# Add, LayerNorm and affine on one core: 16-row loads and stores, each in two transfers of the even and the odd partitions

## The chip, the cores and the metric

The kernel runs on one core of a Trainium2 chip. The metric is the device time of one launch in microseconds (us), the median of several runs. A launch takes about 2 us longer than the span that its profile shows (243.2 us against a span of 241.3 us for the kernel before).

## The reference

```python
def reference(x, residual, gamma, beta, eps):      # x, residual: [16, 1024, 512] float32
    z = x + residual
    mean = np.mean(z, axis=-1, keepdims=True)
    var = np.var(z, axis=-1, keepdims=True)
    z_norm = (z - mean) / np.sqrt(var + eps)
    return (gamma * z_norm + beta).astype(np.float32)
```

There are 16,384 rows of 512 floats. On chip each of the 128 partitions holds 128 of them ("rows 0 to 127" below are the rows of one partition, 2 KB each). Two inputs of 33.55 MB are read and one output of 33.55 MB is written.

## The kernel before

All loads and stores go through one DMA queue, issued by the SyncE (SP) engine. `zbuf` holds 64 rows per partition: x is loaded there, the residual is added in place, the result is made in place, and it is stored from there. So the X load of rows s+64 must wait for the store of rows s. `rbuf` holds 32 rows of the residual. In the code, `P` is the 128 partitions, `D` the 512 floats of a row, `asked`, `added` and `done` count rows, and `STORE_LAG` is by how many rows a store stays behind the X loads that have been issued.

```python
BLOCK = 16
X_CHUNKS = [8] * 15 + [4, 4]
R_CHUNKS = [8] * 15 + [4, 4]
OUT_CHUNKS = [16] * 7 + [8, 4, 4]
GROUP = 4
Z_ROWS = 64
R_ROWS = 32
STORE_LAG = 40
# ... (cut)
def dram(t, lo, n):          # n consecutive rows of every partition: one run of n * 2 KB
    k = lo % BLOCK
    # ... (cut: a check)
    v = t[P * (lo - k) : P * (lo - k + BLOCK), :].rearrange("(p j) d -> p j d", p=P)
    return v[:, k : k + n, :].rearrange("p a b -> p (a b)")
# ... (cut)
def load_x(lo, n):
    nc.sync.dma_start(out=part(zbuf, Z_ROWS, lo, n), in_=dram(xf, lo, n))
def load_r(lo, n):
    nc.sync.dma_start(out=part(rbuf, R_ROWS, lo, n), in_=dram(rf, lo, n))
def store(lo, n):
    nc.sync.dma_start(out=dram(of, lo, n), in_=part(zbuf, Z_ROWS, lo, n))
# ... (cut: add on GpSimd, statistics on ScalarE, affine1 and affine2 on VectorE, 4 rows a group)
def store_due():
    nonlocal added, done
    while stores and (
        stores[0][0] + stores[0][1] <= asked - STORE_LAG or asked == total
    ):
        lo, n = stores.pop(0)
        while done < lo + n:
            added, done = next(steps)
        store(lo, n)

for lo, n in spans(X_CHUNKS):
    asked = lo + n
    # ... (cut: a check)
    load_x(lo, n)
    while loads_r and loads_r[0][0] + loads_r[0][1] <= asked:
        while added < loads_r[0][0] + loads_r[0][1] - R_ROWS:
            added, done = next(steps)
        load_r(*loads_r.pop(0))
    if lo == 0:
        spread()
    store_due()
```

## Time and profile before

| | before |
|---|---|
| median time | 243.16 us (243.11 to 243.18, 3 runs) |
| span of the profile | 241.3 us |
| queue 1 (all loads and stores) | 100.67 MB, 97.9% of 16 engines |
| VectorE, ScalarE, GpSimd busy | 74%, 75%, 60% |

The first lines are from the profile's page of the kernel before. "DMA" and "GB/s" divide the span into 40 slices; the queue lines give packets, megabytes and the share of the 16 DMA engines' time; the "DMA 62%" line is the chain of work that ended last; the GpSimd (POOL) line gives busy us, mean ns, and the idle time before it with what ended most of it; the last two give what is loaded or stored, its issuing queue, how often, the KB each, and the median us from issue to landing.

```profile
span 241.3 us, 1109 instructions
...
DMA  7999999999999999999999999999999999999992
GB/s 261 434 435 434 434 430 418 421 425 432 432 470 436 391 426 421 429 434 426 430 434 437 430 424 429 429 451 410 425 426 432 475 387 418 462 434 432 413 410 117
...
q1 hardware_dynamic: 6336, 100.67, 97.9%
q14 instruction: 9, 0.07, 0.1%
...
DMA 62%; ACT 16%; DVE 6%; POOL 6%; SPq 1%; issue 1%; DVEq 0%; POOLq 0%
...
L120 POOL TENSOR_TENSOR zbuf<-zbuf,rbuf 128x2048 f32<-128x2048 f32 x32 | 144.1, 4526 | 70.6 <-DMA rbuf<-in_residual_dram 69.6
...
zbuf<-in_x_dram SPq DMA_DIRECT2D x15, 2048.0 KB, 29.2
...
out_dram<-zbuf SPq DMA_DIRECT2D x7, 4096.0 KB, 28.6
```

The kernel is bound by its data movement: the DMA engines are busy from end to end, and the first compute engine waits for residual loads, not the reverse.

The next lines are the same kernel's SP engine in order of time (start, duration, what it issued), one period of the loop:

```profile
82.38 0.33 SPq L84 DMA_DIRECT2D zbuf<-in_x_dram  x1
82.80 0.38 SPq L87 DMA_DIRECT2D rbuf<-in_residual_dram  x1
83.28 0.38 SPq L90 DMA_DIRECT2D out_dram<-zbuf  x1
83.71 0.42 SPq L84 DMA_DIRECT2D zbuf<-in_x_dram  x1
84.23 0.39 SPq L87 DMA_DIRECT2D rbuf<-in_residual_dram  x1
```

The period is X, R, S, X, R: behind each store stand an X and a residual load of 2 MB each.

The last lines of before are its windows before the loop's first store lands, in the loop, and after it (start:end, length, busy time of each compute engine, clock, DMA share, GB/s). A whole wave of 16 packets of 32 KB is 0.5 MB, so a window of 120 us can be off by some 4 GB/s, and a short one by much more.

```profile
25.00:75.00 50.00, 0.00 (x0) 0.00 (x0) 49.69 (x82) 49.71 (x153) 45.14 (x11) 1.00 1.02 434
75.00:195.00 120.00, 0.00 (x0) 0.00 (x0) 96.86 (x157) 96.98 (x296) 73.45 (x17) 1.00 1.00 428
195.00:225.00 30.00, 0.00 (x0) 0.00 (x0) 27.76 (x45) 24.48 (x75) 14.29 (x4) 1.00 1.02 433
```

The rate hardly drops where loads and stores are mixed. Between 75 and 195 us no packet starts after a gap (packet records, described below).

Finer readings below are from the trace's packet records (start, duration, size of each packet). They do not name the DMA engine; packets were put on 16 engines by joining each to the one that ended just where it starts. The median packet took 309 ns for 8 KB, 611 to 612 ns for 16 KB and 1213 ns for 32 KB. Where several engines end a packet within a few ns of each other the joining is ambiguous, so what is said of a single engine is less certain than what is said of all 16. "Excess" is a packet's time over the median of its size, per engine (the sum over all packets divided by 16).

### The profile page before, as it was taken

Reading aid. Unit: us, or ns where it says so; the run is one execution under the profiler, and the core shown is the slowest. Engines: PE = TensorE matmul, PEld = TensorE weight load, DVE = VectorE, ACT = ScalarE, POOL = GpSimd, SP = SyncE. Lnnn points to the kernel's source line nnn. Section 1 sums busy time; section 2 is a strip of 40 time slices with the busy share of each in tenths; the row PEclk is TensorE's granted clock in tenths of the full one; section 3 lists DMA queues with packets and bytes.
Section 4 is the critical chain, followed back from the end, with each engine's and each line's share of the span. In section 5 each row is a group of like instructions: output and inputs, shape, how many; then the busy total and the mean of one; then the engine's idle time right before and its main releaser. Section 6 shows DMA issues by size and latency. Waiting matters only on the chain.

```text
span 241.3 us, 1109 instructions
## 1 busy us (share of the span) xinstructions
PE 4.1 (2%) x4; PEld 1.0 (0%) x4; DVE 178.5 (74%) x290; ACT 180.1 (75%) x546; POOL 144.3 (60%) x36
## 2 busy tenths in 40 slices
PE   3300000000000000000000000000000000000000
PEld 0000000000000000000000000000000000000000
DVE  0005999999999999899934999359991699969200
ACT  2009999999999999999709997099961999697000
POOL 0088988989889507894078940889209891860000
DMA  7999999999999999999999999999999999999992
GB/s 261 434 435 434 434 430 418 421 425 432 432 470 436 391 426 421 429 434 426 430 434 437 430 424 429 429 451 410 425 426 432 475 387 418 462 434 432 413 410 117
DMA packets 6349, 100.74 MB, mean 417 GB/s; under 512 B 706, under 2 KB 706, under 8 KB 708
## 3 DMA queue, kind: packets, MB, share of 16 engines
q1 hardware_dynamic: 6336, 100.67, 97.9%
q14 instruction: 9, 0.07, 0.1%
q10 hardware_dynamic: 4, 0.00, 0.0%
HBM read 67.11 MB, written 33.55 MB: 417 GB/s over the span
## 4 chain that ended last, share of the span: by engine, by line
DMA 62%; ACT 16%; DVE 6%; POOL 6%; SPq 1%; issue 1%; DVEq 0%; POOLq 0%
DMA rbuf<-in_residual_dram 34%; DMA out_dram<-zbuf 28%; ACT junk L131 9%; ACT junk L140 7%; POOL zbuf L120 6%; DVE zbuf L175 3%; DVE zbuf L161 3%; SPq L84 1%; ACT std L148 0%; SPq L87 0%; SPq L90 0%; DVEq L261 0%; DVE rstd L173 0%; POOLq L120 0%; DVEq L161 0%
## 5 line engine op out<-in xcount | busy, mean ns | idle before, releaser
L120 POOL TENSOR_TENSOR zbuf<-zbuf,rbuf 128x2048 f32<-128x2048 f32 x32 | 144.1, 4526 | 70.6 <-DMA rbuf<-in_residual_dram 69.6
L161 DVE SCALAR_TENSOR_TENSOR zbuf<-zbuf,nm,gamma_t 128x512 f32<-128x512 f32 x128 | 89.5, 746 | 44.4 <-issue 22.5
L131 ACT ACTIVATE junk<-zbuf 128x512 f32<-128x512 f32 x128 | 74.2, 580 | 38.9 <-POOL zbuf L120 38.9
L175 DVE SCALAR_TENSOR_TENSOR zbuf<-zbuf,rstd,beta_t 128x512 f32<-128x512 f32 x128 | 87.1, 743 | 1.2
L140 ACT ACTIVATE junk<-zbuf,nm 128x512 f32<-128x512 f32 x128 | 85.9, 671 | 0.0
L140 ACT ACTIVATION_READ_ACCUMULATOR junk<-zbuf,nm 128x1 f32 x128 | 24.0, 187 | 0.0
L131 ACT ACTIVATION_READ_ACCUMULATOR junk<-zbuf 128x1 f32 x128 | 23.9, 187 | 0.0
L148 ACT ACTIVATE std<-ssq,eps_t 128x4 f32<-128x4 f32 x32 | 8.5, 267 | 1.0
L173 DVE RECIPROCAL rstd<-std 128x4 f32<-128x4 f32 x32 | 5.6, 175 | 0.0
L186 ACT ACT_TABLE_LOAD x1 | 1.3, 1283 | 1.5 <-PEq L247 1.5
L190 PE MATMUL beta_t<-gb_row,ones 1*128 1x512 f32 x2 | 2.1, 1136 | 2.3 <-DMA gb_row<-in_beta_dram 2.3
L190 PE MATMUL gamma_t<-gb_row,ones 1*128 1x512 f32 x2 | 2.0, 1122 | 2.3 <-DMA gb_row<-in_gamma_dram 2.3
L104 DVE MEMSET ones<- 1x128 f32 x1 | 0.2, 165 | 0.8 <-PEq L247 0.8
L190 PEld LDWEIGHTS beta_t<-gb_row,ones 1*128 1x128 f32 x2 | 0.5, 308 | 3.9 <-DMA gb_row<-in_beta_dram 3.9
L190 PEld LDWEIGHTS gamma_t<-gb_row,ones 1*128 1x128 f32 x2 | 0.5, 308 | 2.2 <-issue 2.2
L247 POOL MEMSET const-float32-0.0<- 128x1 f32 x1 | 0.1, 99 | 0.2 <-issue 0.2
L186 ACT ACTIVATE warm<-eps_t 128x1 f32<-128x1 f32 x1 | 0.2, 203 | 0.0
L247 POOL MEMSET const-bfloat16-1.0<- 128x1 bf16 x1 | 0.1, 102 | 0.0
L247 POOL MEMSET const-uint8-127<- 128x1 uint8 x1 | 0.1, 102 | 0.0
L247 POOL MEMSET const-float32-1.0<- 128x1 f32 x1 | 0.1, 99 | 0.0
L106 DVE MEMSET eps_t<- 128x1 f32 x1 | 0.1, 59 | 0.0
## 6 DMA issues: line engine op xcount, KB each, us to landing
zbuf<-in_x_dram SPq DMA_DIRECT2D x15, 2048.0 KB, 29.2
rbuf<-in_residual_dram SPq DMA_DIRECT2D x15, 2048.0 KB, 29.9
out_dram<-zbuf SPq DMA_DIRECT2D x7, 4096.0 KB, 28.6
zbuf<-in_x_dram SPq DMA_DIRECT2D x2, 1024.0 KB, 32.3
rbuf<-in_residual_dram SPq DMA_DIRECT2D x2, 1024.0 KB, 32.3
out_dram<-zbuf SPq DMA_DIRECT2D x1, 2048.0 KB, 23.5
out_dram<-zbuf SPq DMA_DIRECT2D x2, 1024.0 KB, 16.7
gb_row<-in_gamma_dram ACTq DMA_DIRECT2D x1, 2.0 KB
```

Source lines behind the costliest of these rows:

```text
L84: nc.sync.dma_start(out=part(zbuf, Z_ROWS, lo, n), in_=dram(xf, lo, n))
L104: nc.vector.memset(ones, 1.0)
L120: nc.gpsimd.tensor_tensor(out=z, in0=z, in1=part(rbuf, R_ROWS, j0, n), op=ALU.add)
L131: nc.scalar.activation(out=junk, in_=zrow(j0 + k), func=ACT.Identity, scale=-inv_d, accum_out=nm[:, k : k + 1],)
L140: nc.scalar.activation(out=junk, in_=zrow(j0 + k), func=ACT.Square, bias=nm[:, k : k + 1], accum_out=ssq[:, k : k + 1],)
L148: nc.scalar.activation(out=std[:, :n], in_=ssq[:, :n], func=ACT.Sqrt, bias=eps_t[:, 0:1], scale=inv_d,)
L161: nc.vector.scalar_tensor_tensor(out=zrow(j0 + k), in0=zrow(j0 + k), scalar=nm[:, k : k + 1], in1=gamma_t, op0=ALU.add, op1=ALU.mult,)
L173: nc.vector.reciprocal(out=rstd[:, :n], in_=STD.pop(g)[:, :n])
L175: nc.vector.scalar_tensor_tensor(out=zrow(j0 + k), in0=zrow(j0 + k), scalar=rstd[:, k : k + 1], in1=beta_t, op0=ALU.mult, op1=ALU.add,)
L186: nc.scalar.activation(out=warm, in_=eps_t, func=ACT.Sqrt)
L190: nc.tensor.matmul(dest, ones, gb_row[:, k, :], start=True, stop=True)
L247: nc = _bacc.Bacc("TRN2", target_bir_lowering=False, num_devices=1)
```

## The change

The intent is fewer, larger packets: a packet is one partition's run, and with 16 rows it is 32 KB. A single 4 MB X load would need all of the old store to be out before it starts, so each 16-row transfer is cut into two of 2 MB, one of the even and one of the odd partitions: the even half of a load then waits only for the even half of the store.

```diff
-X_CHUNKS = [8] * 15 + [4, 4]
-R_CHUNKS = [8] * 15 + [4, 4]
+X_CHUNKS = [16] * 8
+R_CHUNKS = [8, 8] + [16] * 6 + [8, 4, 4]
 OUT_CHUNKS = [16] * 7 + [8, 4, 4]
@@
+    def transfer(out, in_, n):
+        parts = 2 if n == BLOCK else 1
+        for h in range(parts):
+            nc.sync.dma_start(out=out[h::parts, :], in_=in_[h::parts, :])
+
     def load_x(lo, n):
-        nc.sync.dma_start(out=part(zbuf, Z_ROWS, lo, n), in_=dram(xf, lo, n))
+        transfer(part(zbuf, Z_ROWS, lo, n), dram(xf, lo, n), n)
```

(`load_r` and `store` are changed in the same way.) The change also moves the order: with X asked for in steps of 16 rows, a lag of 40 is reached at 48. So the store is issued later in the order, right behind the last load before the X load that waits for it.

More of the change, by code (lines that the diff above doesn't have):

```diff
@@ L81, in part @@
         return buf[:, lo % size : lo % size + n, :].rearrange("p a b -> p (a b)")
+    def transfer(out, in_, n):
+        parts = 2 if n == BLOCK else 1
+        for h in range(parts):
+            nc.sync.dma_start(out=out[h::parts, :], in_=in_[h::parts, :])
     def load_x(lo, n):
-        nc.sync.dma_start(out=part(zbuf, Z_ROWS, lo, n), in_=dram(xf, lo, n))
+        transfer(part(zbuf, Z_ROWS, lo, n), dram(xf, lo, n), n)
     def load_r(lo, n):
-        nc.sync.dma_start(out=part(rbuf, R_ROWS, lo, n), in_=dram(rf, lo, n))
+        transfer(part(rbuf, R_ROWS, lo, n), dram(rf, lo, n), n)
     def store(lo, n):
-        nc.sync.dma_start(out=dram(of, lo, n), in_=part(zbuf, Z_ROWS, lo, n))
+        transfer(dram(of, lo, n), part(zbuf, Z_ROWS, lo, n), n)
     def zrow(j):
```

## The prediction

> **What bounds the kernel now.** The data movement. The page's slices show the 16 DMA engines at 90% or more in 38 of 40 slices; queue 1 moves 100.67 MB and is busy 97.9% of the 241.3 us span (queue part). VectorE is busy 74%, ScalarE 75%, GpSimd 60%; the chain of waits is 62% DMA. The compute engines wait for residual loads (69.6 us of GpSimd's idle time), not the reverse.
>
> **Packet cost, from the packet records of the trace.** A packet is one partition's run. Medians: 8 KB 309 ns, 16 KB 612 ns, 32 KB 1213 ns. So two 16 KB packets cost 1224 ns against 1213 ns for one of 32 KB: 11 ns saved per pair. Stores of 16 rows are already 32 KB packets.
>
> **What the change does.** X goes from 1920 packets of 16 KB and 256 of 8 KB to 1024 of 32 KB; the residual trades 1536 of 16 KB for 768 of 32 KB. Saving: X 12 us, residual 8.4 us of engine time, over 16 engines 1.3 us in all. The issues stay near 2 MB each (44 before, 53 after), about 0.4 us of the queue engine each, hidden. Arithmetic is unchanged.
>
> **Waits.** An X load of rows s+64 reuses the buffer of the store of rows s. Before, a store has two 2 MB loads queued behind it (about 9.8 us of DMA work) when the next X load waits for it. After, with the 40-row lag rounded up to 48, that store is the last thing queued, so a single transfer would drain the queue each time. The halves prevent it: the even X load waits only for the even store half, with the odd half (4 packets per engine, 4 x 1213 = 4.85 us) still queued. Landing, wait and issue cost an estimated 2 us (the first packet starts about 1 us after the first issue begins), so that cover should hold. Coarser residual waits (16 rows must be added first, 4 x 4.5 us) lie well inside a period of about 29 us. So on this account: 243.2 - 1.3 = about 242 us.
>
> **The danger.** No transfer before has 64 partitions with step 2, so the trace doesn't show how these spread. [...] I hold the two about equal. The first is a narrow outcome, the second a wide one; my figure is the narrow one.
>
> **What would show it.** Right: 32 KB load packets at about 1213 ns, DMA above 97%, mean about 420 GB/s, no dips. Wrong by collision: load and store packets far above 1213 ns, DMA busy share still high, GB/s falling to 220 to 330 in the middle, and near 430 again where 128-partition transfers end the run. Wrong by drain: packets at 1213 ns, but DMA share dipping once per 29 us where X waits for a store.
>
> **Figures.** 242 us; 8 in 10 between 240.8 and 380. Faster by over 2%: 0.03; within 2%: 0.51; slower by over 2%: 0.46.

The passage cut from "The danger" took no term out of the sum: it stays 243.2 - 1.3 = about 242 us. The passage was a mechanism that no trace of this case shows. It ended in "the two", two outcomes for the packets of the halves: they stay near 1213 ns (the narrow outcome), or they stretch toward twice that (the wide one, called "collision" below it; the name says no more than that). For the wide one, estimated: 300 to 440 us. The upper end can be worked out from the packets: 2688 of 32 KB (88 MB) at 2 x 1213 ns are 408 us over 16 engines, and the other 12.6 MB at 1224 ns for 32 KB are 29 us. That they would stretch, and the lower end, were the author's estimate and not shown. The 220 to 330 GB/s are about 100.67 MB over these times. The range up to 380 us and the 0.46 for slower by over 2% rest on the wide outcome alone.

## More of the kernel before

Note the 29.2 us from issue to landing of an X load: it is long because the load is issued with much other work still queued ahead of it.

The X load at 82.38 us waited for the landing of the store of rows 0 to 15, and its first packet was not needed before 90.3 us (packet records), so it had 7.9 us to start.

## The result and the profile after

| | before | after |
|---|---|---|
| median time, same rounds | 243.17 us (4 runs) | 245.72 us (245.59 to 246.01, 4 runs) |
| ratio | | 1.0107 (95%: 1.0089 to 1.0124) |
| span | 241.3 us | 243.8 us |
| packets of queue 1 | 6336 | 4512 |
| 32 KB packets: median, mean | 1213, 1216 ns | 1213, 1242 ns |
| excess packet time from 75 to 195 us, per engine | 0.49 us | 4.00 us |

A ratio, here and below, is the mean time of one kernel's fast runs over that of the other's of the same rounds, so it is not quite the ratio of the medians quoted. Executions over 1.5% slower than the fastest of the same kernel are left out of the means. The change made the kernel 2.5 us slower; 1.2 us faster had been forecast.

The page of the kernel after, the same lines:

```profile
span 243.8 us, 1105 instructions
...
DMA  7999999999999999999999999999999999999995
GB/s 259 430 417 444 430 430 431 430 430 430 431 435 425 421 430 414 430 387 419 430 421 430 415 419 419 382 430 425 431 419 371 403 402 465 435 435 433 409 410 219
...
q1 hardware_dynamic: 4512, 100.67, 97.9%
q14 instruction: 10, 0.07, 0.1%
...
DMA 69%; POOL 9%; DVE 7%; SPq 4%; POOLq 4%; issue 2%; DVEq 0%
...
L125 POOL TENSOR_TENSOR zbuf<-zbuf,rbuf 128x2048 f32<-128x2048 f32 x32 | 143.7, 4525 | 72.2 <-DMA rbuf<-in_residual_dram 70.0
...
zbuf<-in_x_dram SPq DMA_DIRECT2D x16, 2048.0 KB, 10.2
...
out_dram<-zbuf SPq DMA_DIRECT2D x15, 2048.0 KB, 27.1
```

Arithmetic is unchanged (GpSimd 143.7 us against 144.1), and the DMA share is the same 97.9%. Two things differ: an X load now lands 10.2 us after its issue where it took 29.2 us, so it is issued onto a queue with little left in it; and the share says nothing of the loss, because a stretched packet counts as busy. The windows show it, and where it is:

```profile
25.00:75.00 50.00, 0.00 (x0) 0.00 (x0) 46.26 (x75) 47.65 (x145) 41.46 (x10) 1.00 1.00 431
75.00:195.00 120.00, 0.00 (x0) 0.00 (x0) 100.96 (x164) 101.20 (x310) 77.65 (x18) 1.00 0.99 415
195.00:225.00 30.00, 0.00 (x0) 0.00 (x0) 27.27 (x45) 27.34 (x84) 17.97 (x4) 1.00 1.01 432
```

Between 75 and 195 us, where loads and stores are mixed, the rate is 415 GB/s where it was 428; before and after that stretch it is the same within the coarseness of the view. 120 us x (428 - 415) / 428 is about 3.6 us.

The SP engine of the kernel after, in order of time ("x2" are the two halves):

```profile
60.94 1.11 SPq L86 DMA_DIRECT2D rbuf<-in_residual_dram  x2
62.15 1.18 SPq L86 DMA_DIRECT2D out_dram<-zbuf  x2
87.78 5.35 SPq L86 DMA_DIRECT2D zbuf<-in_x_dram  x2
93.22 1.19 SPq L86 DMA_DIRECT2D rbuf<-in_residual_dram  x2
94.50 1.18 SPq L86 DMA_DIRECT2D out_dram<-zbuf  x2
117.63 5.33 SPq L86 DMA_DIRECT2D zbuf<-in_x_dram  x2
```

After the store's issue at 62.15 us nothing is issued for 24 us: the store is the last thing queued. The X pair is spread over 5.35 us, since each half waits for its half of the store.

The packet records show two losses in each period of about 30 us.

- **Loss A, ahead of the store.** The last one or two packets of the odd residual half just ahead of each of the first four stores are slow on nearly all 16 engines: 0.61, 0.69, 0.56 and 0.37 us in the mean of the engines (at 78 to 81, 108 to 111, 138 to 142 and 168 to 172 us). Before, the same places had 0.11, 0.06, 0.03 and 0.03 us.
- **Loss B, the X load behind the store.** Odd X halves start late: mean gaps of 0.10, 0.11 and 0.33 us (up to 1.99 us on one engine) at rows 64, 96 and 112, and the first packets there are slow by 0.24, 0.60 and 0.51 us, also on engines that had no gap.

What ends the span is a pair of DMA engines that also carry the fetches of the instruction queue (queue 14): 239.66 and 239.78 us before, 242.17 and 242.19 us after, while most others are done some 3 us earlier before and 1 to 2 us earlier after. The account of the one with five fetches in each kernel, in us:

| term | before | after | difference |
|---|---|---|---|
| first packet starts | 2.13 | 2.12 | -0.01 |
| packets at the median of their size, and packets of 4 bytes (704 before, 800 after: 16 for each issue) | 234.69 | 233.67 | -1.01 |
| excess of the first packet of all | 0.41 | 0.74 | +0.33 |
| excess of other packets, up to 0.06 us each | 0.84 | 0.22 | -0.62 |
| excess of other packets, over 0.06 us each | 1.59 | 4.86 | +3.27 |
| instruction fetches | 1.55 | 1.55 | 0 |
| overlaps (a packet starts 3 to 4 ns before the one ahead ends) | -1.42 | -0.99 | +0.43 |
| end | 239.78 | 242.17 | +2.40 |

So fewer packets saved about 1.2 us (-1.01 at the medians, -0.62 of small excess, +0.43 since fewer packets overlap), and 3.3 us of strongly stretched packets took it back. Of those 4.86 us about 2.8 are loss A (0.84, 0.54, 0.85, 0.38, and 0.18 at the fifth store), 1.1 are loss B (0.12, 0.53 and 0.47; this engine had no gaps), and 0.95 lie in the packets just behind its five instruction fetches (0.36, 0.12, 0.25, 0.11, 0.11). Before, 1.25 of the 1.59 us lay just behind the fetches.

### The profile page after: what moved, and what is told of

Same layout as the page of the kernel before. It is cut to its first block, busy times and chain, and to the rows that moved or that the text cites. A ratio compares the mean times of both kernels' runs of the same rounds, so it can differ in the third digit from the quotient of the medians.

```text
span 243.8 us, 1105 instructions
## 1 busy us (share of the span) xinstructions
PE 4.1 (2%) x4; PEld 1.0 (0%) x4; DVE 178.4 (73%) x290; ACT 180.2 (74%) x546; POOL 143.9 (59%) x36
## 3 DMA queue, kind: packets, MB, share of 16 engines
q1 hardware_dynamic: 4512, 100.67, 97.9%
## 4 chain that ended last, share of the span: by engine, by line
DMA 69%; POOL 9%; DVE 7%; SPq 4%; POOLq 4%; issue 2%; DVEq 0%
DMA out_dram<-zbuf 46%; DMA rbuf<-in_residual_dram 20%; POOL zbuf L125 9%; SPq L86 4%; POOLq L266 3%; DVE zbuf L166 3%; DMA zbuf<-in_x_dram 3%; DVE zbuf L180 3%; DVEq L266 0%; DVE rstd L178 0%; POOLq L125 0%
## 5 line engine op out<-in xcount | busy, mean ns | idle before, releaser
L125 POOL TENSOR_TENSOR zbuf<-zbuf,rbuf 128x2048 f32<-128x2048 f32 x32 | 143.7, 4525 | 72.2 <-DMA rbuf<-in_residual_dram 70.0
## 6 DMA issues: line engine op xcount, KB each, us to landing
zbuf<-in_x_dram SPq DMA_DIRECT2D x16, 2048.0 KB, 10.2
```

The costliest lines, as they stand in the source:

```text
L125: nc.gpsimd.tensor_tensor(out=z, in0=z, in1=part(rbuf, R_ROWS, j0, n), op=ALU.add)
```

## The experiments

The theory after the result was: both losses come from the order, since the store is now the last thing in the queue. The rivals were: transfers of 64 partitions are slow at a handover (halves); 32 KB load packets are (size). All 13 runs gave correct results. The stalls quoted are loss A: the mean excess, in us, of the last load transfer ahead of the first, second, third and fourth store, from one profiled execution of each run. Experiments are edits of the kernel after, unless said.

### The changed kernel's order with 16 KB packets

```diff
+        w = (n // parts) * D
-            nc.sync.dma_start(out=out[h::parts, :], in_=in_[h::parts, :])
+            nc.sync.dma_start(out=out[:, h * w : (h + 1) * w], in_=in_[:, h * w : (h + 1) * w])
```

> The order and the 2 MB units of the changed kernel, but each unit is 8 rows of all 128 partitions (16 KB packets) in place of half the partitions. In the changed kernel I count two losses per engine: about 2.5 us in the third packet of the odd residual half, just ahead of a store (A), and about 2.3 us of gaps and slow first packets in X loads that had waited for a store half (B). My theory: A comes from the half-partition transfers, B from the order (the X load waits for the store queued last). Then here B stays (gaps and slow first packets at the second X unit after a store wait, 1.5 to 2.5 us in all), A is gone (under 0.3 us), stores lose the 32 KB packet: 244.5 to 246 us. Rival 1, everything comes from the halves: neither A nor B, about 243.5 us. Rival 2, A comes from the coarser order too: both stay, about 247 us.

Measured: 244.81 us against 243.48, ratio 1.0054 (1.0039 to 1.0070). Stalls 0.03, 0.08, 0.35, 0.19. Its windows' line of the mixed stretch, to compare with 428 and 415 GB/s:

```profile
75.00:195.00 120.00, 0.00 (x0) 0.00 (x0) 104.47 (x170) 103.99 (x317) 72.26 (x17) 1.00 1.00 423
```

The order alone, with two transfers but with all partitions and small packets, already costs time against the kernel before, about half of what the change costs. Loss A is there at two stores and weak at two, so this alone settles neither rival. It also shows that the order isn't all: in the same order, 16 KB packets of all partitions lose 1.9 us per engine between 75 and 195 us where the changed kernel loses 4.00.

### The halves cut at partition 64

```diff
-            nc.sync.dma_start(out=out[h::parts, :], in_=in_[h::parts, :])
+            nc.sync.dma_start(out=out[h * (P // parts) : (h + 1) * (P // parts), :],
+                              in_=in_[h * (P // parts) : (h + 1) * (P // parts), :])
```

> The changed kernel with the halves cut as partitions 0 to 63 and 64 to 127 in place of even and odd. It asks whether the danger of my prediction exists at all. [...] the 32 KB packets of the halves take about 2.4 us against 1.21 us and the kernel takes 400 to 450 us; even and odd was then the right cut[...]. [...] packets stay at 1.21 us and the time at about 246 us.

The words cut are the conditions of the two outcomes, which no trace of this case shows, and one conclusion from them. What is left are the outcomes: the stretched packets that the prediction feared, or packets as even and odd had them.

Measured: 421.63 us against 243.48, one run (a second, 430.81 us, is over 1.5% above it). Lines of its page:

```profile
span 419.9 us, 1105 instructions
...
DMA  9999999999999999999999998999999999999981
GB/s 200 200 372 231 219 228 200 200 206 222 219 203 201 203 309 253 228 237 231 365 237 213 207 228 334 237 209 203 232 318 225 201 197 398 247 276 257 278 300 74
```

The engines are as busy as ever (queue 1 at 96.9%, against 97.9%) and move little more than half the bytes per us (240 GB/s in the mean of the span, against 413, and 197 to 240 in 27 of the 40 slices); the median 32 KB packet took 2465 ns instead of 1213. This is the stretching that the prediction feared. The even and odd halves do not have it: their packets kept 1213 ns, as the stores of all 128 partitions had before. So the cut into even and odd was the right one, and the danger was real only for the other cut. Why the one cut stretches the packets and the other does not, no record here shows.

### A lag of 32: the store issued one step earlier in the order

```diff
-STORE_LAG = 40
+STORE_LAG = 32
```

> The changed kernel with STORE_LAG 32 in place of 40, so each store is issued one step of 16 rows earlier and an X load waits for a store that has at least 8 MB queued behind it. My theory: B (about 2.3 us) goes, A (about 2.5 us) stays: 243 to 244 us, with A still seen as packets of 1.5 to 2 us in the odd residual half ahead of each store. Rival: the waits for the store cost nothing and the halves alone are the loss: 245 to 246 us as before this edit.

Measured: 244.35 us against 243.48, ratio 1.0043 (1.0027 to 1.0059). Stalls 0.61, 0.07, 0.09, 0.04, and no late X halves. Excess from 75 to 195 us is 0.29 us per engine, against 4.00 after. The windows:

```profile
75.00:195.00 120.00, 0.00 (x0) 0.00 (x0) 92.53 (x151) 92.81 (x284) 73.11 (x17) 1.00 1.00 432
195.00:225.00 30.00, 0.00 (x0) 0.00 (x0) 27.37 (x45) 27.41 (x84) 22.94 (x6) 1.00 1.01 431
```

The SP engine, in order of time:

```profile
73.44 1.14 SPq L86 DMA_DIRECT2D out_dram<-zbuf  x2
74.63 1.23 SPq L86 DMA_DIRECT2D zbuf<-in_x_dram  x2
81.35 1.51 SPq L86 DMA_DIRECT2D rbuf<-in_residual_dram  x2
95.84 1.61 SPq L86 DMA_DIRECT2D out_dram<-zbuf  x2
98.22 5.35 SPq L86 DMA_DIRECT2D zbuf<-in_x_dram  x2
```

Losses A and B go, but for A at the first store, when loads stand behind the store (8 MB were queued behind the second to fourth store), with halves and 32 KB packets kept. Between 75 and 195 us no packet starts after a gap. That speaks for the order and against the halves as their cause: my first reading of the trace, that half-partition transfers stall at a handover, fell here. But the time did not come back to that of before. The reason is the end: the last three stores waited for their arithmetic, with mean gaps of 0.3, 0.6 and 2.7 us on the engines (3.6 us in all), where the kernel before had none.

### The same with whole transfers

```diff
-STORE_LAG = 40
+STORE_LAG = 32
-        parts = 2 if n == BLOCK else 1
+        parts = 1
```

> As e7_lag32, but every 16-row load and store is one transfer of 128 partitions (4 MB, 32 KB packets). My theory: neither A nor B; only the saving of 11 ns per pair of packets is left, 241.5 to 242.3 us, faster than both kernels. Rival: the stall A belongs to 32 KB load packets ahead of a store, not to the halves: it stays at about 0.5 us per store and the time is 243.5 to 244.5 us.

Measured: 243.71 us against 243.48, ratio 1.0013 (1.0001 to 1.0026). Stalls 0.70, 0.12, 0.01, 0.07; the last stores again waited, 3.1 us in all. With this lag the halves have nothing left to do, and whole transfers are 0.3% faster than halves on the same chip. The expected gain over the kernel before did not come: A stayed at the first store, and the end had been left out.

### The changed kernel again

No edit.

> The changed kernel once more, unedited. It asks whether the stall A repeats from one execution to the next: in the first profile all 16 DMA engines lost 0.37 to 0.69 us on average in the last two packets of the odd residual half ahead of the stores of rows 0, 16, 32 and 48, 2.2 us in all, with B (late X halves) about 2.3 us. If A belongs to the order of the transfers it comes at the same four places, 0.3 us or more each, and the time is 245.5 to 246.1 us. If A is a chance event of one execution, places and sizes differ.

Measured: 245.55 us against 243.09, ratio 1.0098 (1.0083 to 1.0113). Stalls 0.56, 0.46, 0.72, 0.34. The slowdown and loss A repeat.

### A lag of 32, and stores held back in the second half

```diff
-STORE_LAG = 40
+STORE_LAG = 32
-            stores[0][0] + stores[0][1] <= asked - STORE_LAG or asked == total
+            stores[0][0] + stores[0][1] <= min(asked - STORE_LAG, total // 2)
+            or asked == total
```

> The changed kernel with STORE_LAG 32, and the store of rows 64 to 79 held back until the last loads are issued, as it was with lag 40. In e7_lag32 the gaps B were gone and A came only ahead of the first store, but the last three stores waited for the computation (about 4 us of gaps at the end), so the gain was hidden. My theory: A and B both come from the queue that runs short behind a store, and with the store held at the end nothing hides it: the engine that ends last loses about 1.8 us less to A and 1.1 us less to B, so 242.5 to 243.2 us, the last stores without gaps over 0.3 us. Rival: the halves cost time of their own that e7's tail concealed: 244 us or more, with A at every store.

Measured: 244.44 us against 243.09, ratio 1.0047 (1.0031 to 1.0062). Stalls 0.77, 0.14, 0.10, 0.04. Fewer stores run ahead of the last loads, so the arithmetic of the last rows starts sooner. The mean gaps at the end fell from 3.6 us in all to 1.2, and there is none on the engine that ended last, at 241.23 us. That engine carried five instruction fetches, lost 0.25 to 0.75 us in stretched packets near each or soon after, and 0.76 us of the first-store stall; most others were done at 238.2 us. The time is that of the rival, but A came at the first store alone, so neither expectation held.

### The same with whole transfers

```diff
 (as the edit before, and)
-        parts = 2 if n == BLOCK else 1
+        parts = 1
```

> As e12_lag32_hold, but each 16-row transfer whole, over 128 partitions. If halves as such cost nothing it equals e12 within 0.3 us (9 fewer issues and a first packet 0.3 us earlier favour it): 242.2 to 243 us, about 0.5 us better than the kernel before. If halves cost, it is a microsecond or more faster than e12.

Measured: 243.82 us against 243.09, ratio 1.0024 (1.0011 to 1.0036). Stalls 0.76, 0.15, 0.02, 0.10. Again whole transfers do a little better than halves, though the intervals of the two just overlap; again it is not faster than before. (It has 29 issues where the halves have 50, so 21 fewer and not 9.)

### The store between the X load and the residual load

```diff
     load_x(lo, n)
+        if asked < total:
+            store_due()
     # ... residual loads
-        store_due()
+    store_due()
```

> The changed kernel with the store of each step issued between the X and the residual loads, lag 40 kept. Then a store is followed in the queue by 4 MB of residual loads when the next X load waits for it, and the load packets just ahead of a store are those of the odd X half. Theory 1, A comes when nothing is queued behind the store: A gone or under 0.2 us at stores after the first, B gone. Theory 2, any run of 32 KB load packets stalls when it gives way to a store with 8 MB or less behind it: A moves to the odd X half, 0.4 to 0.7 us each at four stores, B gone. The tail may wait for the computation as in e7_lag32, so the stalls in the trace decide, not the time: 243.5 to 245 us.

Measured: 244.56 us against 243.09, ratio 1.0055 (1.0041 to 1.0068). Stalls 0.67, 0.03, 0.04, 0.00; excess from 75 to 195 us is 0.22 us per engine. The mixed stretch:

```profile
75.00:195.00 120.00, 0.00 (x0) 0.00 (x0) 92.43 (x151) 92.71 (x284) 72.70 (x17) 1.00 1.00 431
```

```profile
84.29 1.19 SPq L86 DMA_DIRECT2D out_dram<-zbuf  x2
85.53 1.23 SPq L86 DMA_DIRECT2D rbuf<-in_residual_dram  x2
107.97 5.33 SPq L86 DMA_DIRECT2D zbuf<-in_x_dram  x2
```

This keeps the lag, the halves and the packets and moves only 4 MB of residual load behind the store. Losses A and B go at the second to fourth store; no packet starts after a gap between 75 and 195 us. This is the cleanest sign that they belong to what is queued behind the store. The end is compute's again: most engines ended at 238.3 us, against about 236.6 before, and the last at 240.6 us.

### The residual in two transfers of 8 rows

```diff
-        transfer(part(rbuf, R_ROWS, lo, n), dram(rf, lo, n), n)
+        for k in range(lo, lo + n, 8):
+            transfer(part(rbuf, R_ROWS, k, min(n, 8)), dram(rf, k, min(n, 8)), min(n, 8))
```

> The changed kernel with only the residual loads returned to two transfers of 8 rows over 128 partitions, so the packets just ahead of each store are 16 KB; X and stores keep their even and odd halves, order and lag as in the changed kernel. Theory 1, the stall A needs 32 KB load packets just ahead of a store: A falls under 0.2 us per engine and store (it was 0.4 to 0.7), B stays, 243.2 to 244.3 us. Theory 2, A comes from the order alone (nothing queued behind the store): A stays at 0.4 us or more at four stores and the time at 245.5 us or more.

Measured: 246.74 us against 243.36, ratio 1.0136 (1.0115 to 1.0157). Stalls 0.15, 0.60, 0.28, 0.40. The transfer that stalls is now of 128 partitions in 16 KB packets, and it stalls still at the second to fourth store. So loss A needs neither halves nor 32 KB packets in the load ahead of the store (X loads and stores still have both here). The stall at the first store, however, went.

### The residual whole

```diff
-    def transfer(out, in_, n):
-        parts = 2 if n == BLOCK else 1
+    def transfer(out, in_, n, whole=False):
+        parts = 2 if n == BLOCK and not whole else 1
-        transfer(part(rbuf, R_ROWS, lo, n), dram(rf, lo, n), n)
+        transfer(part(rbuf, R_ROWS, lo, n), dram(rf, lo, n), n, whole=True)
```

> The changed kernel with the 16-row residual load whole over 128 partitions, 32 KB packets, all else as in the changed kernel. If A depends on 32 KB load packets and not on half partitions, it stays at 0.4 to 0.7 us at four stores: 245 to 246 us. If the half-partition residual load makes it, A goes: 243 to 244 us.

Measured: 246.21 us against 243.36, ratio 1.0116 (1.0100 to 1.0132). Stalls 0.47, 0.77, 0.71, 0.49. The whole transfer stalls as much as the half, so the half partitions of the residual don't make the loss.

### The kernel before with the residual in 16 rows

An edit of the kernel before:

```diff
-R_CHUNKS = [8] * 15 + [4, 4]
+R_CHUNKS = [8, 8] + [16] * 6 + [8, 4, 4]
```

> The kernel before with only its residual loads as whole 16-row transfers of 32 KB packets (first two and last three as in the changed kernel). Each store then follows an X load of 16 KB packets and has 6 MB or more behind it when an X load waits for it. My theory: no A over 0.1 us, no B; the saving is that of the residual alone, 0.3 us: 242.7 to 243.1 us. Rival, any 32 KB load packets cost time somewhere: 243.5 us or more.

Measured: 243.37 us against 243.36, ratio 0.9999 (0.9987 to 1.0012). Stalls 0.63, 0.06, 0.02, 0.02. In the old order, with 6 MB behind the stores, 32 KB load packets bring the stall of the first store only. What the larger packets save is not seen in the time, and the first store's stall was not expected.

### Whole transfers, lag of 32, held stores, residual in 8 rows

```diff
 (as the whole transfers with held stores, and)
-        transfer(part(rbuf, R_ROWS, lo, n), dram(rf, lo, n), n)
+        for k in range(lo, lo + n, 8):
+            transfer(part(rbuf, R_ROWS, k, min(n, 8)), dram(rf, k, min(n, 8)), min(n, 8))
```

> e13_whole_hold with the residual loads by 8 rows, so 32 KB packets only in X and stores, and 16 KB packets just ahead of every store, with a deep queue behind it. In e13 the first store cost every engine about 0.7 us, and the two engines that also carry instruction fetches lost about 1.3 us more than in the kernel before. Theory 1 of e15: both vanish, leaving the X saving of about 0.4 us: 242.4 to 243 us, at or just below the kernel before. Theory 2: as e13, 243.6 us or more.

Measured: 243.90 us against 243.36, ratio 1.0025 (1.0013 to 1.0038). Stalls 0.46, 0.06, 0.06, 0.03. This was tried as a version that might beat both. It does not.

### Four small loads behind each store of the changed kernel

Is it the bytes behind the store that matter, or that something is queued there? The loads read 16 rows of x again into a tile that nothing uses.

```diff
+    fill = consts.tile([P, 4, D], FP32)
@@ (after store(lo, n) in store_due)
+            if asked < total:
+                for f in range(4):
+                    nc.sync.dma_start(out=fill[0:16, f, :], in_=xf[0:16, :])
```

> The changed kernel with four small loads of 32 KB in all (16 partitions of 2 KB, into a tile that nothing reads) queued behind each pair of stores in the loop: four more transfers stand behind each store, but only 0.125 MB, 0.05 us or so of queue time on each engine. If the stall just ahead of a store goes away because of the number of transfers queued behind the store, it is below 0.2 us at the second to fourth store and the time falls towards 244.5; if it takes megabytes behind it (time in which the queue is not near its end), the stall stays at 0.4 to 0.7 us and the time is 245.5 to 246.5. The late X halves (0.1 to 0.3 us of gap) stay either way, since X still waits for the store.

Measured: 247.30 us against 243.26, ratio 1.0162 (1.0119 to 1.0204; its runs spread from 246.13 to 248.02). The engines could not be followed one by one past 92 us here, so the sums over all 16 were taken in fixed windows. Ahead of the first store the stall is still there (0.81 us). Ahead of the second to fourth store the excess is 0.07, 0.06 and 0.10 us where the changed kernel has 0.69, 0.56 and 0.37: loss A is gone there, with 0.125 MB added behind each store. But the stall is not saved, it moved: the first packets of the X load behind the small loads now lose 0.59, 0.62, 0.58 and 0.52 us, where the changed kernel's even halves lose 0.02 to 0.14 in the same windows. The excess from 75 to 195 us is 3.61 us per engine in all, against 4.00. The windows agree, and the SP engine shows the order:

```profile
75.00:195.00 120.00, 0.00 (x0) 0.00 (x0) 100.69 (x163) 100.94 (x308) 77.36 (x18) 1.00 1.00 417
```

```profile
62.35 1.33 SPq L87 DMA_DIRECT2D out_dram<-zbuf  x2
63.72 8.88 SPq L226 DMA_DIRECT2D fill<-in_x_dram  x4
88.33 5.55 SPq L87 DMA_DIRECT2D zbuf<-in_x_dram  x2
```

The small loads were not as cheap as expected: their 256 packets of 2 KB took a median of 84 ns, which is 1.3 us per engine over the run and not 0.05 us for each store. That is about what the run is slower than the changed kernel; without it the time would be near 246.0 us (an estimate from these two numbers).

Both expectations were half right: loss A follows the number of transfers queued behind the store, as the first said, but the time did not fall, since about 0.6 us per period is lost at the X load instead. This fits the reading that the loss at the second to fourth store comes with a queue that runs near its end, and that which packets are stretched depends on what stands there. The stall of the first store doesn't fit it.

## Why the prediction was right or wrong

**What held.** The kernel is bound by its DMA engines, before and after (97.9% busy). The packet costs were right: 32 KB packets stayed at a median of 1213 ns, in loads and in stores. Their saving, forecast as "over 16 engines 1.3 us in all", is about 1.2 us in the account above. That it comes so close is partly luck: the forecast left out that packets overlap (0.43 us less) and that small excess falls (0.62 us more). The issues number 50 after and not 53, which changes nothing. The arithmetic is unchanged, and no cost of the coarser residual waits is seen. The narrow outcome for the halves came, with their packets at 1213 ns; the cut at partition 64 shows that halves can have stretched packets, of 2465 ns, at 422 us. That even and odd escape this was not foreseen but held "about equal". The most probable class, within 2%, and the range held, but the range was so wide (up to 380) because of the wide outcome, and says nothing for the account of the waits.

**The step that failed** is "Landing, wait and issue cost an estimated 2 us (the first packet starts about 1 us after the first issue begins), so that cover should hold." It put the cost of the waits at zero. Loss A and loss B are about 3.9 us on an engine that ends last (2.8 and 1.1 us), and with them the saving of 1.2 us became a loss of 2.4 to 2.5. The account failed in two ways, and the second is the larger.

1. *The cover was mis-sized.* The 4.85 us were counted on one engine. Here a store had landed only when the slowest of the 16 engines was done, and the next load was needed by the fastest. The even half of the first store ended at 85.76 us on the first engine and at 87.38 on the last; X was issued at 87.78. The odd half's last packet ended at 92.22 us, the odd X half was issued at 92.6, and the leading engine wanted it at 95.45: 2.8 us were left of 4.85. At rows 96, the odd half was issued at 152.93 us and wanted at 155.16: 2.2 us. And the start of a transfer was not 1 us on every engine: at the changed kernel's start the first packet came 1.36 us after the first issue began on the first engine (2.09 - 0.73), 2.43 us on the last (3.16 - 0.73); in the kernel before it was 1.01 and 1.93 us. Counted from the end of the issuing instruction it was less on the first engine (0.63 us before, 0.77 after); but the cover has to hold for the last engine, with the issue counted in. So the odd halves came too late on some engines: the one issued at 92.6 us had its first packet on one engine only at 96.72, 4.1 us after the issue, and the one issued at 183.23 on one engine at 187.03, 3.8 us after. The gaps, 0.5 us in the mean of the engines, are this step. That the slow first packets (1.4 us in the mean) are its doing too is argued from their going together with the gaps in the two orders that keep loads behind the store.
2. *The stretched packets were not foreseen at all.* I looked for gaps only. The prediction's sign for a drain, "DMA share dipping once per 29 us where X waits for a store", was the wrong sign: the share stayed 97.9%, and the loss stood in packets of up to 2.4 us and in the GB/s. Loss A falls ahead of the store, before any X load waits for that store.

**What the runs settle.** Both losses need the order, in which the store is the last thing queued: but for the first store's stall they are gone in both orders that put loads behind it (lag of 32, store ahead of the residual), with halves and packets unchanged; and loss A stays with the residual in small packets or in whole transfers, so the form of the load ahead of the store doesn't make it. How large the losses are depends on the packets too: with 16 KB packets of all partitions in the same order they are about half (1.9 against 4.00 us of excess). Packet size and half partitions were both changed there, and which of the two doubles the loss was not tested. The cover that the halves give is not enough for this order. And the halves are themselves not free, for a reason that was not looked for: where the queue is deep enough without them, whole transfers were 0.3% (lag 32) and 0.2% (held stores) faster.

**Why no repaired version wins.** Without losses A and B about 1 us should remain. By the traces three things take it, though none was removed alone to test this: a stall of 0.5 to 0.8 us at the first store, which came in all versions with 32 KB loads but one; the end of the run, where earlier stores push the last loads back and the last store then waits for arithmetic (3.6 and 3.1 us in the kernels with a lag of 32); and, once that is relieved, the engines that carry instruction fetches, which are 2 to 3 us behind the others (as they are in the kernel before). The best of these, whole transfers at a lag of 32, was 0.1% slower than the kernel before (1.0001 to 1.0026).

**What stays open.** What the DMA engine does in the stretched packets is not shown by any record. That the stall moved with four small loads says that it depends on what is left in the queue, not how. Why the first store of the run stalls even with 4 MB and more behind it was not found, nor why a residual in 8 rows took this stall away in one order (0.15 us) and not in another (0.46 us); nor why the packet just behind an instruction fetch loses 0.09 to 0.66 us (before and after) beside the 0.31 us of the fetch itself.

## What to carry to other kernels

When a load waits for a store on the same queue, count the cover from the landing on the slowest engine to the need of the fastest (here 2.2 to 2.8 us were left of 4.85), and keep other loads queued behind the store: here 4 MB behind it were enough for all stores but the first, and a second half of 2 MB was not. Changing a chunk size also changes the order when a lag is counted in rows, so look at the order of issues first; here it cost about 3.9 us where the packets saved 1.2. In a DMA-bound kernel read GB/s and packet durations, since here the busy share did not show that packets stretched: it was 97.9% before and after, and 96.9% where the kernel took 422 us.
